# Keys per head in place of queries times the keys' weights, and scores of two heads on the two halves of TensorE's rows

## The chip, the cores and the metric

The kernel runs on one core of one Trainium2 chip. The metric is the device time of one execution in microseconds (us), taken as the median of several runs. The core has five engines that work side by side and wait for one another through semaphores: PE (TensorE, matmuls; its weight loads are listed as PEld), DVE (VectorE), ACT (ScalarE), POOL (GpSimd) and SP (SyncE, which issues most DMAs). Matmuls write to PSUM, which has eight banks of 128 rows x 512 words here; the other operands lie in SBUF.

## What is computed

One decoder layer on 1024 rows of width 1024: a gated network (SwiGLU), a token mixer, and a second gated network, each with a residual and a layer norm. The change lies in the mixer's attention, and in the first network where it prepares the mixer's weights. In the reference:

```python
proj = h @ w_in
q, c, qi, ki, wi, z = jnp.split(proj, SPLITS, axis=-1)   # q: 8 heads x 64
c = _rmsnorm(c, kv_norm_g)                               # latent keys, 128 wide
q_abs = jnp.einsum('blhd,hcd->blhc', q, w_uk) * 64 ** -0.5
sc = jnp.einsum('bqhc,bqkc->bqhk', q_abs, c_sel)         # the 256 keys that the indexer picks
p = jax.nn.softmax(sc, axis=-1)
o_lat = jnp.einsum('bqhk,bqkc->bqhc', p, c_sel)
att = jnp.einsum('bqhc,hcd->bqhd', o_lat, w_uv)
```

The selection is carried out as a bias: each row's 256th largest indexer score is found bit by bit (top-k), and keys below it get a bias of -2^100, so that the softmax runs over all keys up to the causal limit. The score of a head is q (64 wide) times `w_uk` (64 x 128) times c (128 wide); the product may be taken from either side.

## The kernel before

Numbers are kept to about 22 bits by splitting each operand in a high and a low part (`split`, L84: ACT copies the rounded high part, DVE subtracts it to get the low part) and adding three products: high x high, high x low, low x high (`mm3`, L148). `mm2` (L698) does the same with two products where one operand has its high and low part stacked on the 128 rows.

The instructions of an engine are put in order by a planner with a model of their times. It takes what is ready, the earlier in the program first, and can bring a later instruction far forward if its buffer is free. Buffers come from pools: `page` (21 of 128 x 1024 words), `big` (15 of twice that size; `large` and `both` take from it), `w` (2, taken by `raw`), and in PSUM `one` (4 single banks) and `two` (2 double banks). Buffers of a pool are given out in the order of the program, and a buffer is free again when the last reader is done.

The first network runs over 11 groups of hidden columns; a group has five to seven products of 24 matmuls (`product`, L314). From group 2 on, each quarter of a product takes one step of `make_parts` (L99). This generator loads 29 blocks of mixer weights one after another into `w` buffers, splits them on ACT and DVE and stores the parts to HBM. A network's own weights for group g + 1 are loaded while group g runs (L341).

The mixer (L1078) then projects. For the queries, `queries` (L959) projects four heads' columns at a time (`proj_t`) and `stack` (L689) puts a head's high part on one half of the rows and, by a DMA that POOL issues, its low part on the other half. Heads 0 to 3 are done before the product of the gated part with the output weights, heads 4 to 7 behind it. `latent` (L748) norms the latent keys, splits them (`ch`, `cl`) and transposes them (`cT`); its transposes stand behind the last queries. `q_abs` (L967) multiplies the stacked queries with `wuk` and splits the result over the buffers of `act` (eight `big` buffers, no longer needed by then).

The attention (L1015) goes over 16 jobs: pairs of row blocks 0 to 3, in each two groups of four heads, in each the two blocks. For a job, `softmax` (L978) runs per head: three matmuls per chunk of up to 512 keys into a double bank, one DVE reduction that adds the bias and finds the maximum (L993), one exponential with its sum (L995), a reciprocal, and a scaling on POOL (L997). Two heads' `p` share a `big` buffer. Then `attend` (L1000) takes the job before: for each block of keys four transposes of `p`, a split, and three matmuls with the latent keys into `ol`. Behind each two jobs `heads` (L1026) multiplies with `wuv`. The output weights `wo` (four `big` buffers) are loaded behind the ninth job (L1066). Top-k steps are pumped between all of these (`pump`); blocks 4 to 7 end their top-k with an equality mask `eq`, a scan `rank` and an update of the bias (L874 to L885).

Of the kernel before, what the change touches and what calls it, by code (L numbers as in the profile page):

```python
# [34 lines left out]
class Net:  # L35
# [63 lines left out]
    def make_parts(self):  # L99
# [9 lines left out]
        todo += [("wuk", flat(ins["w_ukT"]))]  # L109
# [146 lines left out]
    def ffn(self, name, w13, w2, begin, meanwhile, load_acc, norm, after, side=iter(())):  # L256
# [57 lines left out]
        def product(g, m, ps, start=True):  # L314
            now = plan.index((g, m))
            for k in range(4):
# [12 lines left out]
                if g > 1 and now > 2 * EARLY:  # L329
                    next(side, None)  # L330
# [322 lines left out]
    def w_uk(self):  # L653
        self.wuk = self.load_w("wuk", "wuk", (P, NH, P))

# [142 lines left out]
    def topk(self, blocks, plan):  # L798
# [64 lines left out]
        for i in sorted(blocks):  # L863
# [12 lines left out]
            eq = self.page("eq", (P, 1024), BF16)[:, :n]  # L876
            rank = self.page("rank")[:, :n]
# [81 lines left out]
    def queries(self, j):  # L959
        w = self.load_t(j)  # L960
        two = [self.page("q", dt=F32R) for _ in range(2)]
        lo = self.page("ql", dt=F32R)
        for h in range(2):
            self.stack(two, self.proj_t(w, 4 * h, 4), lo, slice(h * HALF, (h + 1) * HALF))
        return two

    def q_abs(self, q):  # L967
        self.w_uk()
        for h in range(2):
            for head in range(NH):  # L970
                ps = self.bank("qa")
                self.mm2(ps, q[head][:, h * HALF : (h + 1) * HALF], [x[:, head] for x in self.wuk], True)
                if PAR["QA"][8 * h + head]:
                    self.split_far(ps, *self.act_cols(4 * h, 4, head))
                else:
                    self.split(ps.rearrange("p (t c) -> p t c", t=4), *self.act_cols(4 * h, 4, head))

    def softmax(self, i, head):  # L978
        nc, V = self.nc, self.nc.vector
        s = (i + 1) * P  # L980
        n, w = self.chunks(s)
        ps = self.banks("sc")
        for j in range(n):
            ks = slice(j * w, (j + 1) * w)
            self.mm3(ps[:, j * HALF : j * HALF + w], self.act_tile(i, head), (self.cT[0][:, ks], self.cT[1][:, ks]), True, True)
        if head % 2 == 0:
            self.pp = self.large("p", (P, 2, 1024), F32)
        p = self.pp[:, head % 2]
        m, l = self.small("m", 1), self.small("l", 1)
        view = ps.rearrange("p (j c) -> p j c", j=2)[:, :n, :w]  # L990
        pv = p[:, : n * w].rearrange("p (j c) -> p j c", j=n)
        bv = self.bias[i].rearrange("p (j c) -> p j c", j=n)
        V.tensor_tensor_reduce(pv, view, bv, -1.0, 3.0e38, ALU.add, ALU.min, m)  # L993
        p = p[:, :s]
        nc.scalar.activation(p, p, AF.Exp, bias=m, scale=-1.0, accum_out=l)  # L995
        V.reciprocal(l, l)
        self.engine(PAR["PN"][head % 4]).tensor_scalar(p, p, l, 0.0, ALU.mult, ALU.add)  # L997
        return p
# [16 lines left out]
    def attention(self, x1, norm, after):  # L1015
# [10 lines left out]
        def heads(pair, hg):  # L1026
            if hg == 0:
                attT[pair] = [self.page("at", (P, 4, 2, P), F32R) for _ in range(2)]
# [26 lines left out]
        for n, job in enumerate([(pair, hg, b) for pair in PAR["O"] for hg in range(2) for b in range(2)]):  # L1055
# [4 lines left out]
            for hh in range(4):  # L1060
                ready[job].append(self.softmax(2 * pair + b, 4 * hg + hh))
# [16 lines left out]
    def mixer(self, x1, tail, norm, after):  # L1078
# [54 lines left out]
        q = []  # L1133
        for j in range(2):
            q.extend(self.queries(j))
            for i in range(2):
                self.to_gmT(4 + 2 * j + i)
            self.pump(PAR["Q"][j])
        wo = self.load_wout(1)
        for t in range(NT):  # L1140
# [5 lines left out]
            self.pump(PAR["W"][t])  # L1146
        for j in range(2, 4):
            q.extend(self.queries(j))
            self.pump(PAR["Q"][j])
            if PAR["L"] == j:  # L1150
                self.latent(craw)
        if PAR["L"] == 4:
            self.latent(craw)
        self.q_abs(q)
# [31 lines left out]
def layouts(i):  # L1186
# [23 lines left out]
    uk = i["w_uk"][0].transpose(2, 0, 1)  # L1210
# [23 lines left out]
```

## Time and profile before

| | us |
|---|---|
| median of 3 runs | 1782.01 (1781.88 to 1782.98) |
| profiled execution | 1782.18 |
| its span | 1780.5 |
| PE busy | 1728.8 (97%) |
| DVE busy | 1330.2 (75%) |
| ACT busy | 792.0 (44%) |
| POOL busy | 394.1 (22%) |

The profile is taken on one execution. A busy share is an average over stages with different limits: the first network runs from 0 to about 640 us, the mixer to about 1150, the second network to the end. A matmul's own row gives the time from its start to its last output, 0.39 us for 512 columns, and such rows overlap; what a stream of them costs is read from the distance of their starts. The granted clock of PE is a share of 2.4 GHz; it has two levels, 1.0 and 0.5 of that, and a stretch shows a mean. Idle time in brackets is that of the engine just before the instruction, with what ended it.

### The profile page before, as it was taken

The page shows a single profiled execution, that of the slowest core. Times are in us where ns is not written, and L with a number is a line of the kernel's source. Part 1 is how long each engine was busy: PE and PEld are TensorE (multiplying, and loading weights), DVE is VectorE, ACT ScalarE, POOL GpSimd, SP SyncE. Part 2 cuts the span into 40 slices and gives each one's busy share as a digit, 9 for nine tenths or more (in the row PEclk, how much of TensorE's full clock was granted, in tenths as well). Part 3 has the DMA queues.
Part 4 walks back from the last instruction along what each step waited for, and adds up shares of the span by engine and source line. Part 5 has one row for each costly group of instructions (what it writes and reads, how often), then busy time and mean ns, then how long its engine had stood idle before and what let it go on. Part 6 is the DMA issues. An engine that isn't in the chain of part 4 may idle for free.

```text
span 1780.5 us, 22284 instructions
## 1 busy us (share of the span) xinstructions
PE 1728.8 (97%) x8056; PEld 1449.9 (81%) x8056; DVE 1330.2 (75%) x2213; ACT 792.0 (44%) x1328; POOL 394.1 (22%) x287
## 2 busy tenths in 40 slices
PE   8989999999999999999978999999999999999997
PEld 6878888888888889998866888888788888888886
DVE  5778886765895864699889877877877555589586
ACT  5433333333654524568687662452313222354551
POOL 0004332222000460011246421100423222200036
PEclk9999999999999999999999999999999999999999
DMA  7458777758545342225412006435443322753532
GB/s 285 154 213 318 256 262 276 280 204 305 192 122 173 107 184 95 96 84 198 169 36 95 1 1 212 154 119 188 157 178 121 136 89 89 288 195 118 181 101 83
DMA packets 90141, 289.96 MB, mean 163 GB/s; under 512 B 9136, under 2 KB 9648, under 8 KB 85680
## 3 DMA queue, kind: packets, MB, share of 16 engines
q1 hardware_dynamic: 82496, 253.12, 40.1%
q10 hardware_dynamic: 5616, 32.54, 4.6%
q0 software_dynamic: 1920, 2.89, 0.8%
q8 instruction: 63, 1.03, 0.2%
q14 instruction: 46, 0.38, 0.1%
HBM read 195.94 MB, written 89.69 MB: 160 GB/s over the span
## 4 chain that ended last, share of the span: by engine, by line
PE 71%; DVE 7%; ACT 4%; DMA 2%; issue 2%; POOL 1%; SPq 0%; POOLq 0%; ACTq 0%; DVEq 0%
PE ab L151 11%; PE ab L153 11%; PE ab L152 11%; PE y L152 5%; PE y L153 5%; PE y L151 5%; PE z L153 3%; PE z L152 3%; PE z L151 3%; ACT act L828 2%; PE pN L153 2%; PE pN L151 2%; PE pN L152 2%; PE tr L1006 1%; PE lg L702 1%
## 5 line engine op out<-in xcount | busy, mean ns | idle before, releaser
L151 PE MATMUL ab<-xs,hi 128*128 128x512 f32 x1232 | 482.4, 392 | 18.4 <-DVE c L415 6.7
L152 PE MATMUL ab<-xs,hi 128*128 128x512 f32 x1232 | 481.2, 391 | 0.0
L153 PE MATMUL ab<-xs,lo 128*128 128x512 f32 x1232 | 481.0, 391 | 0.0
L151 PEld LDWEIGHTS ab<-xs,hi 128*128 128x128 f32 x1232 | 232.6, 189 | 69.7 <-issue 12.5
L152 PEld LDWEIGHTS ab<-xs,hi 128*128 128x128 f32 x1232 | 232.6, 189 | 48.9 <-DVE xs L88 0.4
L153 PEld LDWEIGHTS ab<-xs,lo 128*128 128x128 f32 x1232 | 232.5, 189 | 48.6
L88 POOL TENSOR_TENSOR lo<-w,hi 128x1024 fp32r<-128x1024 f32 x54 | 137.9, 2553 | 568.6 <-ACT hi L87 531.2
L87 ACT ACTIVATE hi<-w 128x1024 fp32r<-128x1024 f32 (+1 forms) x134 | 137.6, 1040 | 160.4 <-DVE w L290 126.6
L88 DVE TENSOR_TENSOR lo<-w,hi 128x1024 fp32r<-128x1024 f32 (+1 forms) x80 | 94.7, 1195 | 42.4 <-ACT hi L87 41.9
L88 DVE TENSOR_TENSOR a<-hid,a 128x512 fp32r<-128x512 f32 x132 | 93.3, 707 | 24.2 <-ACT a L87 24.0
L87 ACT ACTIVATE a<-hid 128x512 fp32r<-128x512 f32 x132 | 82.0, 621 | 53.9 <-DMA hid<-f 50.2
L153 PE MATMUL z<-b,a 128*128 128x512 f32 x264 | 102.7, 389 | 0.0
L152 PE MATMUL y<-b,a 128*128 128x512 f32 x264 | 102.7, 389 | 0.0
L153 PE MATMUL y<-b,a 128*128 128x512 f32 x264 | 102.7, 389 | 0.0
L152 PE MATMUL z<-b,a 128*128 128x512 f32 x264 | 102.7, 389 | 0.0
L151 PE MATMUL z<-b,a 128*128 128x512 f32 x264 | 102.5, 389 | 0.0
L88 DVE TENSOR_TENSOR b<-w,b 128x512 fp32r<-128x512 f32 x110 | 77.1, 701 | 34.0 <-ACT b L87 33.8
L828 ACT ACTIVATE act<-score,tk 128x768 int8<-128x768 f32 (+2 forms) x93 | 87.0, 935 | 34.2 <-DVE tk L840 27.7
L151 PE MATMUL y<-b,a 128*128 128x512 f32 x264 | 102.0, 389 | 0.0
L87 ACT ACTIVATE b<-w 128x512 fp32r<-128x512 f32 x110 | 68.4, 622 | 51.9 <-PE z L153 38.5
L348 ACT ACTIVATE h<-c 128x512 f32<-128x512 f32 x34 | 21.4, 631 | 152.8 <-DVE c L415 103.3
L592 POOL TENSOR_TENSOR xacc<-xacc,T 128x512 f32<-128x512 f32 x8 | 13.0, 1652 | 333.8 <-DVE T L565 333.8
(264 smaller groups left out, 3586.7 us busy)
## 6 DMA issues: line engine op xcount, KB each, us to landing
w<-in_ffn_w_dram SPq DMA_DIRECT2D x110, 512.0 KB, 6.3
hid<-f SPq DMA_DIRECT2D x60, 512.0 KB, 3.8
w<-in_ffn_w_dram SPq DMA_DIRECT2D x22, 1024.0 KB, 10.3
made<-made ACTq DMA_DIRECT2D x17, 1024.0 KB, 6.3
f<-h SPq DMA_DIRECT2D x32, 512.0 KB, 3.6
f<-c SPq DMA_DIRECT2D x22, 512.0 KB, 3.1
wo<-made SPq DMA_DIRECT2D x8, 1024.0 KB, 6.9
xr<-x_spill SPq DMA_DIRECT2D x16, 512.0 KB, 5.6
```

Source lines behind the costliest of these rows:

```text
L87: nc.scalar.activation(hi, src, AF.Copy)
L88: (eng or nc.vector).tensor_tensor(lo, src, hi.bitcast(F32), ALU.subtract)
L151: mm(out, a[0], b[0], start=start, stop=False, skip_group_check=skip)
L152: mm(out, a[0], b[1], start=False, stop=False, skip_group_check=skip)
L153: mm(out, a[1], b[0], start=False, stop=stop, skip_group_check=skip)
L348: nc.scalar.activation(t, c[:, 0], AF.Silu)
L592: nc.gpsimd.tensor_tensor(acc[j][:, HALF:], acc[j][:, HALF:], T[j], ALU.add)
L702: self.nc.tensor.matmul(out, l, r, start=n == 0, stop=n == 1)
L828: nc.scalar.activation(out, s, AF.Sign, bias=fj, scale=-1.0, accum_out=val[:, j : j + 1])
L1006: nc.tensor.transpose(pt[:, hh * P : (hh + 1) * P], ps4[hh][:, j * P : (j + 1) * P], self.ident)
```

## The change

- `queries` no longer stacks: it only splits a projection, and pair j of heads gives one high and one low array, in which head 2j lies on rows 0 to 63 and head 2j + 1 on rows 64 to 127. For j above 1 the two share a `big` buffer.
- A new function `keys` multiplies the latent keys with `w_uk` (laid out so that again two heads share the 128 rows; half as many words to split and store) and splits the result: four pairs, one `big` buffer each. `q_abs`, `w_uk` and the `far` splits are gone.
- `softmax` works on a pair of heads. For each chunk of keys it issues six matmuls, alternately on rows 0 to 63 and 64 to 127, into two double banks (or, up to 512 keys, the two banks of one).
- `latent` stands ahead of the last two query projections.
- `eq` and `rank` take `w` buffers in place of pages; the attention outputs of pairs 0 and 1 take `big` buffers.
- The steps of `make_parts` begin with group 4 in place of group 2.

```diff
-                if g > 1 and now > 2 * EARLY:
+                if g > 3 and now > 2 * EARLY:
                     next(side, None)
...
-            eq = self.page("eq", (P, 1024), BF16)[:, :n]
-            rank = self.page("rank")[:, :n]
+            eq = self.raw("eq").bitcast(BF16)[:, :n]
+            rank = self.raw("rank")[:, :n]
...
     def queries(self, j):
         w = self.load_t(j)
-        two = [self.page("q", dt=F32R) for _ in range(2)]
-        lo = self.page("ql", dt=F32R)
+        q = self.both("q") if j > 1 else [self.page("q", dt=F32R) for _ in range(2)]
         for h in range(2):
-            self.stack(two, self.proj_t(w, 4 * h, 4), lo, slice(h * HALF, (h + 1) * HALF))
-        return two
+            s = slice(h * HALF, (h + 1) * HALF)
+            self.split(self.proj_t(w, 4 * h, 4), q[0][:, s], q[1][:, s])
+        return q
-    def q_abs(self, q):
...
+    def keys(self):
+        w = self.load_w("wuk", "wuk", (P, 4, P))
+        self.k = [self.both("k") for _ in range(4)]
+        for j in range(4):
+            for h in range(2):
+                s = slice(h * HALF, (h + 1) * HALF)
+                ps = self.bank("k")
+                self.mm3(ps, [x[:, j] for x in w], [x[:, s] for x in self.cT], True, True)
+                self.split(ps, *(x[:, s] for x in self.k[j]))
-    def softmax(self, i, head):
+    def softmax(self, i, j):
...
+        two = [self.banks("sc") for _ in range(n)]
+        view = [(x if n == 2 else two[0][:, e * HALF : (e + 1) * HALF]).rearrange("p (j c) -> p j c", j=n)[:, :, :w] for e, x in enumerate((two * 2)[:2])]
+        for c in range(n):
+            ks = slice(c * w, (c + 1) * w)
+            for m, (a, b) in enumerate(((0, 0), (0, 1), (1, 0))):
+                for e in range(2):
+                    r = slice(64 * e, 64 * e + 64)
+                    nc.tensor.matmul(view[e][:, c], self.q[j][a][r, tl], self.k[j][b][r, ks], start=m == 0, stop=m == 2)
+        pp = self.large("p", (P, 2, 1024), F32)
...
-                attT[pair] = [self.page("at", (P, 4, 2, P), F32R) for _ in range(2)]
+                if pair < 2:
+                    attT[pair] = self.both("at", (P, 4, 2, P))
+                else:
+                    attT[pair] = [self.page("at", (P, 4, 2, P), F32R) for _ in range(2)]
...
+        self.latent(craw)
         for j in range(2, 4):
-            q.extend(self.queries(j))
+            self.q.append(self.queries(j))
             self.pump(PAR["Q"][j])
-            if PAR["L"] == j:
-                self.latent(craw)
...
-        self.q_abs(q)
+        self.keys()
         self.w_uv()
```

## Rows read from the trace of the kernel before

**Rows 1.** Part 1 of the page: busy us, share, instructions, of two engines.
```profile
PE 1728.8 (97%) x8056; PEld 1449.9 (81%) x8056; DVE 1330.2 (75%) x2213; ACT 792.0 (44%) x1328; POOL 394.1 (22%) x287
```
**Rows 2.** Windows: stretch, its length, busy time of each engine, clock, DMA.
```profile
core 0: us, PE busy (x) PEld busy (x) DVE busy (x) ACT busy (x) POOL busy (x), PEclk, DMA share, GB/s
905.00:917.00 12.00, 3.88 (x18) 2.77 (x17) 10.96 (x28) 10.31 (x19) 5.17 (x7) 0.81 0.22 44
917.00:966.00 49.00, 41.40 (x216) 32.18 (x215) 43.91 (x141) 39.15 (x105) 30.42 (x37) 0.98 0.07 18
966.00:1084.00 118.00, 114.78 (x684) 99.55 (x684) 93.76 (x189) 77.45 (x150) 38.31 (x39) 1.00 0.13 44
1500.00:1600.00 100.00, 100.00 (x443) 82.81 (x442) 69.81 (x96) 41.87 (x67) 12.23 (x5) 1.00 0.58 211
120.00:130.00 10.00, 6.38 (x29) 4.94 (x27) 5.71 (x5) 1.79 (x2) 0.00 (x0) 1.00 0.52 209
130.00:140.00 10.00, 8.40 (x25) 6.70 (x26) 8.94 (x6) 4.84 (x6) 6.79 (x3) 0.66 0.56 204
```
**Rows 3.** What PE waited for, 640 to 1160 us: total, times, longest.
```profile
PE qa L702 <- DVE ql L694: 8.1, 2, 5.4
PE sc L151 <- DVE m L993: 4.3, 8, 1.3
```
**Rows 4.** Timeline, 909 to 917 us: start, duration, instruction, idle time before.
```profile
909.89 0.73 PE L702 MATMUL qa<-q,wuk 128*128 128x512 f32 x2 [2.70 <-DVE ql L694]
...
911.32 1.23 DVE L88 TENSOR_TENSOR cl<-c,ch 128x1024 fp32r<-128x1024 f32 x1 [0.42 <-ACT ch L87]
...
915.30 0.69 DVE L694 TENSOR_TENSOR ql<-pT,q 128x512 fp32r<-128x512 f32 x1
...
916.04 1.22 PE L702 MATMUL qa<-q,wuk 128*128 128x512 f32 x2 [5.42 <-DVE ql L694]
```
**Rows 5.** The chain that ended last, 966 to 1084 us, by line.
```profile
by line: PE tr L1006 20.0%; PE ol L151 11.6%; PE ol L152 11.2%; PE ol L153 11.1%; PE sc L151 9.1%; PE sc L153 8.8%; PE sc L152 8.8%; PE at L151 2.2%; DVE pT L88 2.0%; PE at L153 2.0%; PE at L152 2.0%; DVE p L993 1.9%; DVE rank L880 1.6%; AC
```
**Rows 6.** Groups by line and form, 905 to 1150 us: busy us, mean ns.
```profile
L88 DVE TENSOR_TENSOR pT<-tr,pT 128x512 fp32r<-128x512 f32 x72 | 48.2, 684 | 11.4 <-ACT pT L87 11.2
...
L993 DVE CUSTOM_DVE_ANT_0 p<-sc,bias 128x1024 f32<-128x1024 f32 x8 | 9.8, 1221 | 3.1 <-PE sc L153 2.0 <-PE tr L1006 1.0
...
L995 ACT ACTIVATE p<-p,m 128x1024 f32<-128x1024 f32 x8 | 9.2, 1153 | 4.2 <-DVE l L996 2.4 <-DVE m L993 1.7
...
L997 POOL TENSOR_SCALAR p<-p,l 128x1024 f32<-128x1024 f32 x8 | 9.0, 1126 | 12.3 <-DVE l L996 12.3
...
L88 DVE TENSOR_TENSOR act<-qa,act 128x512 fp32r<-128x512 f32 x13 | 8.9, 687 | 0.9 <-ACT act L87 0.6
...
L993 DVE CUSTOM_DVE_ANT_0 p<-sc,bias 128x640 f32<-128x640 f32 x8 | 6.5, 812 | 0.0
```
**Rows 7.** Timeline of PE, 1004 to 1008 us, transposes and scores of blocks 5 and 6.
```profile
1004.01 0.60 PE L1006 MATMUL tr<-ident,p 128*128 128x128 f32 x4
1004.37 0.42 PE L151 MATMUL sc<-cTh,act 128*128 128x384 f32 x1
1004.63 0.34 PE L152 MATMUL sc<-cTl,act 128*128 128x384 f32 x1
1004.81 0.35 PE L153 MATMUL sc<-cTh,act 128*128 128x384 f32 x1
...
1005.72 0.37 PE L152 MATMUL sc<-cTl,act 128*128 128x448 f32 x1
1005.93 0.37 PE L153 MATMUL sc<-cTh,act 128*128 128x448 f32 x1
```
**Rows 8.** Timeline of SP's queue, 955 to 980 us.
```profile
963.09 9.42 SPq L145 DMA_DIRECT2D wo<-made  x4
```
**Rows 9.** Timelines of SP's queue, DVE and PE, 75 to 140 us.
```profile
82.02 20.28 SPq L116 DMA_DIRECT2D made<-in_w_inT_dram  x3
...
124.19 1.23 DVE L287 TENSOR_TENSOR S<-w,w 128x1024 f32<-128x1024 f32 x1 [7.29 <-DMA w<-in_ffn_w_dram]
...
131.60 0.76 PE L151 MATMUL ab<-xs,hi 128*128 128x512 f32 x1 [5.22 <-DVE c L415]
```

More of the change, by code (lines that the diff above doesn't have):

```diff
@@ L651, in gate_consts @@
         nc.sync.dma_start(self.glg[:, 1], ins["gmlp_ln_b"].partition_broadcast(P))
-    def w_uk(self):
-        self.wuk = self.load_w("wuk", "wuk", (P, NH, P))
     def w_uv(self):
@@ L960, in queries @@
         w = self.load_t(j)
-        two = [self.page("q", dt=F32R) for _ in range(2)]
-        lo = self.page("ql", dt=F32R)
+        q = self.both("q") if j > 1 else [self.page("q", dt=F32R) for _ in range(2)]
         for h in range(2):
-            self.stack(two, self.proj_t(w, 4 * h, 4), lo, slice(h * HALF, (h + 1) * HALF))
-        return two
-    def q_abs(self, q):
[L968 to L976, printed above, removed]
-    def softmax(self, i, head):
+            s = slice(h * HALF, (h + 1) * HALF)
[11 more added lines that the diff above has]
+    def softmax(self, i, j):
         nc, V = self.nc, self.nc.vector
@@ L981, in softmax @@
         n, w = self.chunks(s)
[L982 to L998, printed above, removed]
+        tl = slice(i * P, (i + 1) * P)
+        two = [self.banks("sc") for _ in range(n)]
[7 more added lines that the diff above has]
+        pp = self.large("p", (P, 2, 1024), F32)
+        out = []
+        for e in range(2):
+            p = pp[:, e]
+            m, l = self.small("m", 1), self.small("l", 1)
+            pv = p[:, : n * w].rearrange("p (j c) -> p j c", j=n)
+            bv = self.bias[i].rearrange("p (j c) -> p j c", j=n)
+            V.tensor_tensor_reduce(pv, view[e], bv, -1.0, 3.0e38, ALU.add, ALU.min, m)
+            p = p[:, :s]
+            nc.scalar.activation(p, p, AF.Exp, bias=m, scale=-1.0, accum_out=l)
+            V.reciprocal(l, l)
+            nc.gpsimd.tensor_scalar(p, p, l, 0.0, ALU.mult, ALU.add)
+            out.append(p)
+        return out
     def attend(self, i, hg, ps4, olat, pending):
@@ L1059, in attention @@
             ready[job] = []
-            for hh in range(4):
-                ready[job].append(self.softmax(2 * pair + b, 4 * hg + hh))
+            for j in range(2):
+                ready[job] += self.softmax(2 * pair + b, 2 * hg + j)
             self.pump(PAR["A"][4 * pair + 2 * hg + b])
@@ L1132, in mixer @@
         self.gate(1, vn1)
-        q = []
+        self.q = []
         for j in range(2):
-            q.extend(self.queries(j))
+            self.q.append(self.queries(j))
             for i in range(2):
@@ L1146, in mixer @@
             self.pump(PAR["W"][t])
+        self.latent(craw)
         for j in range(2, 4):
-            q.extend(self.queries(j))
+            self.q.append(self.queries(j))
             self.pump(PAR["Q"][j])
-            if PAR["L"] == j:
-                self.latent(craw)
-        if PAR["L"] == 4:
-            self.latent(craw)
-        self.q_abs(q)
+        self.keys()
         self.w_uv()
```

5 lines of the change are left out of this document (2 added, 3 removed).

## The prediction

> **What bounds the kernel now.** The shares of busy time were read first. PE is busy for 1728.8 of 1780.5 us and DVE for 1330.2 [rows 1], so time is won only where PE idles, or where PE's own work shrinks and nothing else comes late in its place. The windows then give the stages around the change, and three of them matter [rows 2]. From 905 to 917 us, between the last query projection and the first scores, PE is busy for 3.9 of 12 us at a mean granted clock of 0.81. From 917 to 966 (scores and attention of blocks 0 to 3) PE has 41.4 of 49 us and DVE 43.9. From 966 to 1084 (blocks 4 to 7) PE has 114.8 of 118 us and DVE 93.8. For scale, a stretch in which PE does nothing but 128x512 products holds 443 matmuls in 100 us, so one costs 0.226 us in a stream [rows 2], whatever longer duration its own row shows.
>
> The waits say what the hole is: the product of the queries with the keys' weights (`qa`) waited 8.1 us in two pieces for `ql`, the low part of the queries [rows 3]. The timeline shows the two pieces: `qa` sat idle 2.70 us before 909.89 and 5.42 us before 916.04, where it followed the DVE subtraction at 915.30 by a fraction of a us; DVE and ACT were full of top-k steps in between. The pair at 916.04 took 1.22 us against 0.73 us for the pair before it [rows 4]: PE had idled, and the granted clock of 0.81 is a mean of the two levels, 1.2 and 2.4 GHz. In the stage from 966 on, the chain that ended last is PE: the three lines of the scores alone hold 9.1 + 8.8 + 8.8 = 26.7% of 118 us, 31.5 us [rows 5].
>
> **The change part by part.** *Queries.* The stacking goes: for each of 8 half projections one 64-row ACT copy and two DMAs issued by POOL (16 in all). What stays is one ACT copy and one DVE subtraction. All of it sits beside PE's projections except in the last projection, where it is the 8.1 us hole. Nothing of the new kernel asks PE to wait there: `keys` needs only the latent transposes, which the change puts ahead of the last two projections, and the scores of the first pair need queries that were ready long before. I count the hole as gone, 8.1 us, and 0.5 us for the pair at the lower clock.
>
> *Keys for queries times weights.* 32 `qa` matmuls go and 24 `k` matmuls come (4 pairs x 2 halves x 3), 8 x 0.226 = 1.8 us less PE work. On DVE 13 subtractions (8.9 us) go and 8 come, at 0.684 us for the same shape 5.5 us [rows 6]. The latent subtraction at 911.32 (1.23 us, [rows 4]) moves ahead into a stage where PE is late. What is late next from 905 to 966 is DVE: today 10.96 + 43.91 = 54.9 us of 61, afterwards 54.9 - 8.9 + 5.5 - 1.2 = 50.3. In 61 - 8.6 = 52.4 us it would be 96% full. So 8.6 us is about all that this stage can give; the bounds are 5.1 us (if DVE stays at today's 90%, 55.9 us) and 10.7 us (DVE never idle).
>
> *Scores on two halves.* The matmul count stays: chunks x 3 x 8 heads, 48 for each of blocks 4 to 7. Today each uses all 128 rows of PE. The spacing of two starts is 0.18 us at 384 columns and 0.21 at 448 [rows 7], 0.226 at 512, and about 0.148 at 320 by the same slope: 48 x (0.148 + 0.177 + 0.205 + 0.226) = 36 us of PE work in the last stage. No row shows a matmul on half of the rows. The bounds are that two such matmuls take turns (36 us, nothing gained) and that they stream together (18 us). I take 18: the nearest row is one full matmul, which today streams as many rows and columns in one spacing as the pair does together, and the pair's outputs lie in different PSUM banks. The Trainium skill, TensorE: Matmul & The Clock Gate, section LDWEIGHTS, puts a weight load at 128 columns over 1.2 GHz, 107 ns whatever its rows; as an estimate from that page two loads cost 0.213 us for a pair, so the narrow pairs would not get below that and the 18 us would be 21. No row here separates this, since a load now always lies beside a full matmul.
>
> Each run of half-row matmuls changes what PE does. The nearest row is a change from transposes to scores: the first matmul then takes 0.26 us to the next start instead of 0.18 [rows 7], 0.08 us more. With 16 pairs in the last stage and a change at each end this is 32 x 0.08 = 2.6 us; the upper bound is one full pass of the pipeline, 0.34 - 0.18 = 0.16 us, at 64 changes (each run of six on its own): 10 us. The Trainium skill, TensorEngine Tiling (Array Packing), section Key Properties, speaks against the change here: changing the tiling mode drains TensorE. By it the 10 us would stand in place of the 2.6; the 0.08 us row shows that a change costs something, not that it is a drain.
>
> PE work from 966 on is then 114.8 - 18 + 2.6 = 99.4 us, and DVE keeps 93.8.
>
> *Buffers.* This is what stands against the gain. Of 15 `big` buffers the new kernel holds 4 for keys, 2 for the late queries, 1 for `wuv`, 2 for the attention outputs of pairs 0 and 1, and, from the ninth job on, 4 for `wo` (today loaded from 963.09 on, just as block 4 starts, [rows 8]). Two are left for `p`, which is one job of four heads; today it is 15 - 1 - 4 - 4 = 6. So jobs 9 to 15 can fill `p` only after the job before has been transposed. One job's softmax, from the first reduction to the last scaled head, is for block 7 four reductions 4 x 1.22, the second pair's matmuls 6 x 0.226, one exponential 1.15 and one scaling 1.13 [rows 6]: 8.6 us. For block 4, by the reduction's 0.812 / 1.221, it is 5.7, and the seven jobs add up to 51.5 us (6.7 + 5.7 + 6.7 + 7.6 + 8.6 + 7.6 + 8.6). The transposes follow, and what trails them lies under the next softmax: four PSUM banks let about three groups of splits and value products trail. A job's turn is so 8.6 + 1.7 (a first group: four transposes 0.60 [rows 7], then ACT and DVE, estimated at 1.1 together) + 5 x 0.684 = 13.7 us for block 7 and 5.7 + 1.7 + 2 x 0.684 = 8.8 for block 4; jobs 9 to 15 take 81 us, and about 95 with job 8 and the tail. PE (99), DVE (94) and this turn (95) are then nearly level, and three that wait on one another will not keep PE at today's 97%. I take 93%: 99.4 / 0.93 = 107 us in place of 118, a gain of 11. The bounds are 94 us (DVE never idle) and 133 us (below, as a rival).
>
> `eq` and `rank` move into the two `w` buffers, so each top-k end waits for the one before; the blocks that come last, 6 and 7, are needed only from job 12 on. I cost it at nothing, hidden by jobs 8 to 11; without that cover it is one pass of DVE over a block, which the reduction of the same width puts near 1.2 us.
>
> *Splits begin with group 4.* Today the first weight load of these splits is issued at 82.02 us, and with the later ones it competes with the group's own loads: DVE idles 7.29 us for `w` before 124.19, and PE then waits 5.22 us before 131.60 [rows 9]. The windows 120 to 130 and 130 to 140 hold 29 and 25 matmuls, the second at a clock of 0.66, where 10 us at full speed hold 44.3: (15.3 + 19.3) x 0.226 = 7.8 us lost [rows 2]. But the splits' place in the program is group 2, and the wait at 131.60 (on L415) still belongs to group 1: the first load went out some 50 us or more ahead of its place, with nothing but a free `w` buffer to wait for, and the buffers are the same after the change. I take 0 and keep -7.8 us as a bound. On the other side, if the splits do start ten products later (240 x 0.226 = 54 us), they end as much later, nearer to the network's second half.
>
> **The sum.** The profiled execution took 1782.18 us (span 1780.5 and 1.7 around it), 0.2 above the median of 1782.01. 1782.2 - 8.6 - 11 = 1762.6 us.
>
> **The rivals.** (C) The splits do start late enough that the stall around 131.60 is gone too: 1762.6 - 7.8 = 1754.8. For it speaks that the stall follows a late DMA; against it, the early issue at 82.02. (E) The three limits of the last stage overlap better, 97% for PE (102.5 us) or DVE's 94: 1758 to 1750. (B) The two halves take turns: PE keeps its 115 us, the stage its 118, and only the hole is won: 1773.6. Nothing in the trace speaks for or against it, as no half-row matmul is there. (F) As B, with a full pass lost at 64 changes, 10 us of which the present 3 us of idle time hide a part: 118 + 7 = 125, so 1780.6, no change. This is also how it would look if the change did not do what it says. (D), on the other side: the two `p` buffers make softmax and attention strictly alternate. Then PE's work without scores, 114.8 - 36 = 79, and the softmax turns of 51.5 add up, with 2.6 for changes, to 133 us, 15 more than today: 1782.2 - 8.6 + 15 = 1788.6, slower. It decides if less than about a third of each softmax lies over the trailing splits and products of the job before; for it speaks the count of buffers, against it that four PSUM banks let three groups trail.
>
> **How the numbers follow.** My forecast 0.40, C 0.17, E 0.10, B 0.13, F 0.06, D 0.14. A measurement of this kernel can tell about 0.2%, 3.6 us, from no change. Faster is the forecast, C, E and B, 0.80; the same is F, 0.06; slower is D, 0.14. The range leaves out D and F, 0.20, and reaches on the low side to C and E together with DVE never idle, 1750 - 7.8 = 1742, rounded in to 1743; its upper end of 1779 lies above B.
>
> **What would show it.** Right: no wait of PE for a query between the last projection and the first scores, and no clock below 1.0 there; starts of half-row matmuls in pairs, a pair in about 0.23 us at 512 columns; the stage from block 4 on near 107 us with PE busy well below 97%; waits of DVE's reductions for a `p` buffer, that is for transposes, from the ninth job on. Wrong: half-row starts 0.2 us apart each (B); the stage over 120 us with DVE and PE both below 75% (D); no late `w` load before group 2 in the first network (C). The prediction fails most easily in the last stage, where the gain is a difference of limits that lie close together.

## The result, and the profile after

The changed kernel takes 1796.88 us (median of 4 runs, 1794.75 to 1798.86) beside 1782.43 us for the kernel before on the same chip: a ratio of 1.0082, 95% interval 1.0069 to 1.0094. It is 14.5 us slower; the forecast was 19.4 us faster. The profiled execution has a span of 1795.0 us.

Part 1 of the page, to be read beside [rows 1]: PE is busy 11.8 us longer than before, with 8 matmuls fewer.

```profile
PE 1740.6 (97%) x8048; PEld 1444.7 (80%) x8048; DVE 1328.6 (74%) x2208; ACT 782.2 (44%) x1309; POOL 387.5 (22%) x268
```

Windows of the kernel after, beside [rows 2]. The first line is the hole of before (3.88 of 12 us at clock 0.81): it is full now, at full clock. The last stage runs from 966 to 1098 instead of 1084 (the first product of the output projection starts at 1098.5, before at 1084.5). PE is busy for 95% of it, a little more than the 93% of the forecast, but over 132 us in place of 107; DVE is busy for 65%, where it had been 79%.

```profile
core 0: us, PE busy (x) PEld busy (x) DVE busy (x) ACT busy (x) POOL busy (x), PEclk, DMA share, GB/s
905.00:917.00 12.00, 12.00 (x58) 9.02 (x57) 11.12 (x31) 8.93 (x17) 5.55 (x2) 1.00 0.00 1
917.00:966.00 49.00, 36.69 (x195) 24.82 (x191) 44.97 (x134) 33.32 (x92) 35.35 (x39) 0.83 0.00 1
966.00:1098.00 132.00, 125.71 (x669) 97.46 (x670) 85.65 (x179) 76.23 (x146) 33.51 (x35) 0.96 0.16 55
```

The waits of PE, 640 to 1160 us, beside [rows 3]: the wait for `ql` is gone, and none as large has come. The 14 us can't be found in this list.

```profile
PE sc L989 <- DVE m L997: 6.4, 6, 2.1
PE ol L151 <- ACT pT L87: 4.5, 7, 0.8
PE sc L989 <- DVE tk L879: 2.2, 1, 2.2
PE tr L763 <- DVE xr L952: 2.0, 1, 2.0
```

The timeline of PE shows the keys right behind the last query projection (compare [rows 4]) and, in the last stage, the half-row matmuls of block 6 (compare [rows 7]). The six of one head stand as a run, then a value product, then the six of the other head. Six take 1.49 us, the same 0.2 us per start as full rows had.

```profile
910.26 0.39 PE L153 MATMUL pT<-act,wT 128*128 128x512 f32 x1
910.49 0.39 PE L151 MATMUL k<-cTh,wuk 128*128 128x512 f32 x1
...
1051.42 1.49 PE L989 MATMUL sc<-k,q 64*128 64x448 f32 x6
1052.85 0.49 PE L151 MATMUL ol<-pT,ch 128*128 128x512 f32 x1
1053.27 1.48 PE L989 MATMUL sc<-k,q 64*128 64x448 f32 x6
1054.68 0.50 PE L152 MATMUL ol<-pT,ch 128*128 128x512 f32 x1
1055.03 0.40 PE L153 MATMUL ol<-pT,cl 128*128 128x512 f32 x1
1055.26 0.60 PE L1011 MATMUL tr<-ident,p 128*128 128x128 f32 x4
```

SP's queue and PE in the first network, beside [rows 9]: the first load of the splits is issued at 81.47 us (82.02 before), and the stall at L415 stays.

```profile
81.47 11.14 SPq L116 DMA_DIRECT2D made<-in_w_inT_dram  x2
...
PE ab L151 <- DVE c L415: 4.9, 1, 4.9
```

Three places in time divide the loss. The query projections end at 910.7 us (906.3 before), the first scores start at 912.6 (917.1), the output projection at 1098.5 (1084.5); from there to the end both kernels take 696 us. So 4.4 us come ahead of the attention, 8.9 us are won in the hole, and 18.5 us are lost between the first scores and the output projection.

A fourth place says where. The first scores of block 4, 320 columns wide, start at 965.22 us before and at 956.71 after. The windows run from there to the output projection, before and after:

```profile
965.22 0.31 PE L151 MATMUL sc<-cTh,act 128*128 128x320 f32 x1
965.20:1084.50 119.30, 116.08 (x692) 100.76 (x691) 94.65 (x193) 78.53 (x151) 39.11 (x39) 1.00 0.14 47
```
```profile
956.71 0.52 PE L989 MATMUL sc<-k,q 64*128 64x320 f32 x2 [0.51 <-DVE m L997]
956.70:1098.50 141.80, 134.20 (x718) 104.25 (x719) 93.99 (x195) 82.49 (x161) 36.08 (x38) 0.96 0.15 53
```

At block 4 the changed kernel is still 8.5 us ahead. It has put off some matmuls of blocks 0 to 3 (9 transposes, 7 value products and 12 products with `wuv`, 3.8 us by their usual distances). Behind this place it loses 22.5 us, with the same work on DVE.

### The profile page after: what moved, and what is told of

It reads as the page before. It is cut to its first block, busy times and chain, and to the rows that moved or that the text cites. A ratio compares the mean times of both kernels' runs of the same rounds, so it can differ in the third digit from the quotient of the medians.

```text
span 1795.0 us, 22187 instructions
## 1 busy us (share of the span) xinstructions
PE 1740.6 (97%) x8048; PEld 1444.7 (80%) x8048; DVE 1328.6 (74%) x2208; ACT 782.2 (44%) x1309; POOL 387.5 (22%) x268
## 4 chain that ended last, share of the span: by engine, by line
PE 71%; DVE 7%; DMA 3%; POOL 3%; ACT 2%; issue 2%; SPq 0%; POOLq 0%; ACTq 0%; DVEq 0%
PE ab L151 11%; PE ab L152 11%; PE ab L153 11%; PE y L151 4%; PE y L153 4%; PE y L152 4%; PE z L153 2%; PE z L151 2%; PE z L152 2%; PE pN L153 2%; PE pN L151 2%; PE sc L989 2%; PE pN L152 2%; PE tr L1011 2%; PE pT L151 1%
## 5 line engine op out<-in xcount | busy, mean ns | idle before, releaser
L151 PE MATMUL ab<-xs,hi 128*128 128x512 f32 x1232 | 481.8, 391 | 17.4 <-DVE c L415 6.8
L152 PE MATMUL ab<-xs,hi 128*128 128x512 f32 x1232 | 480.9, 391 | 0.0
L153 PE MATMUL ab<-xs,lo 128*128 128x512 f32 x1232 | 480.7, 390 | 0.0
L152 PEld LDWEIGHTS ab<-xs,hi 128*128 128x128 f32 x1232 | 232.3, 189 | 48.3 <-DVE xs L88 0.4
L153 PEld LDWEIGHTS ab<-xs,lo 128*128 128x128 f32 x1232 | 232.2, 189 | 48.4 <-DVE lo L88 0.2
L87 ACT ACTIVATE hi<-w 128x1024 fp32r<-128x1024 f32 (+1 forms) x134 | 137.6, 1039 | 161.8 <-DVE w L290 124.1
L152 PE MATMUL y<-b,a 128*128 128x512 f32 x264 | 102.7, 389 | 0.0
L153 PE MATMUL y<-b,a 128*128 128x512 f32 x264 | 102.7, 389 | 0.0
L152 PE MATMUL z<-b,a 128*128 128x512 f32 x264 | 102.7, 389 | 0.0
L153 PE MATMUL z<-b,a 128*128 128x512 f32 x264 | 102.7, 389 | 0.0
L816 DVE TENSOR_SCALAR_CACHE_REDUCE dve<-score,tk 128x640 int8<-128x640 f32 (+3 forms) x96 | 84.5, 880 | 0.4
## 6 DMA issues: line engine op xcount, KB each, us to landing
w<-in_ffn_w_dram SPq DMA_DIRECT2D x22, 1024.0 KB, 11.3
```

Of the source, the lines that this page charges most:

```text
L87: nc.scalar.activation(hi, src, AF.Copy)
L151: mm(out, a[0], b[0], start=start, stop=False, skip_group_check=skip)
L152: mm(out, a[0], b[1], start=False, stop=False, skip_group_check=skip)
L153: mm(out, a[1], b[0], start=False, stop=stop, skip_group_check=skip)
L816: V.tensor_scalar(self.marks("dve", s.shape[-1]), s, f, None, ALU.is_lt, ALU.add, accum_out=val[:, j : j + 1])
```

## The experiments

Times are medians in us; each ratio is against the kernel before on the same chip. "The stage" is the time from the end of the query projections to the start of the output projection. For it, each matmul's time from its start to the next start was added up from the single rows of the trace, idle gaps of PE apart (before, e10 and e12 have 8 transposes of latents, 1.0 us, among theirs):

```
kernel            time    ratio [95%]              stage   scores  transposes  values  PE idle
before          1782.4    1                        178.1    56.6     28.2       54.4     18.9
after           1796.9    1.0082 [1.0069, 1.0094]  187.8    54.9     36.3       61.6     18.6
e1_alternate    1793.5    1.0053 [1.0036, 1.0069]  186.8    42.2     39.7       63.9     24.8
e4_full_rows    1788.5    1.0034 [1.0023, 1.0044]  180.5    57.4     30.4       57.7     19.1
e5_wo_last      1787.4    1.0025 [1.0015, 1.0035]  179.4    55.5     33.4       60.5     13.5
e6_alt_wo       1776.1    0.9966 [0.9954, 0.9979]  168.2    41.7     33.0       60.6     16.4
e7_full_wo      1777.3    0.9972 [0.9961, 0.9982]  169.7    57.4     28.7       54.4     13.3
e10 (before)    1794.0    1.0068 [1.0051, 1.0084]  188.5    57.3     30.4       55.6     24.7
e11_same_half   1792.4    1.0055 [1.0040, 1.0070]  183.9    64.7     34.0       60.2      7.9
e12 (before)    1782.6    1.0002 [0.9992, 1.0011]  178.3    57.1     28.5       54.0     17.9
```

**Do the halves meet? (e1)**

```
+        with self.tc.manual_schedule(engines={mybir.EngineType.PE}):
             for c in range(n):
                 ...
                         nc.tensor.matmul(view[e][:, c], ...)
```

> The changed kernel, with the score matmuls of one softmax call held in the order of the program on PE, so that the two heads' halves alternate from matmul to matmul; nothing else differs. Theory 'order': for blocks 4 to 7 the planner issues the six matmuls of one head as a run and the six of the other later, so that the halves seldom meet. If that is why nothing was gained, the starts of half-row matmuls come in pairs, a pair in about 0.23 us at 512 columns and 0.2 at 448, the 39 us of score matmuls in blocks 4 to 7 fall to about 20, and the kernel takes 1780 to 1785 us. Rival 'turns': the two halves can't stream together, the spacing of two starts stays 0.2 us at 448 columns, and the time stays at 1795 to 1799 us. Rival 'limit': the starts pair up, but the p buffers and DVE set the stage, and the time stays within 4 us of 1797.

Measured: 1793.5 us. The starts do pair up, as forecast in the prediction (0.20 us a pair at 448 columns, 0.23 at 512), and the score matmuls fall from 54.9 to 42.2 us. But PE's idle time and the lower clock (0.76 to 0.90 in windows of 20 us from 980 to 1040 us) take nearly all of it: the stage is 1 us shorter. 'Order' is right about the halves and wrong about the time; 'limit' is what the time says. 'Turns' falls.

**What the p buffers cost (e5, e12, e10).** The first two edits are one number, on either kernel; the third holds four buffers in the kernel before.

```
e5, e12:  -'WJ': 8   +'WJ': 16
e10:       wo = self.load_wout(0)
          +held = [self.large("held", (P, 2, 1024), F32) for _ in range(4)]
          +for x in held: nc.sync.dma_start(x[:, 0, :64], ...)
           ...
          +if n == 15:
          +    for x in held: nc.gpsimd.tensor_tensor(..., x[:, 0, :1], ready[job][3][:, :1], ALU.add)
```

> The changed kernel, with the load of the output weights at the end of the attention in place of behind its ninth job, so that four more big buffers stay free for p in jobs 9 to 15. Theory 'p buffers': with two p buffers the softmax of jobs 9 to 15 waits for the transposes of the job before; freed, the stage from block 4 on falls from about 127 us to 118 or less, and the output projection starts with a wait of up to 10 us for its weights (4 loads of 9.7 us beside one another, if nothing else hides them): 1788 to 1797 us, with the wait named. Rival 'no limit': the p buffers are not what PE waits for, the stage stays within 2 us, and the wait for the weights comes on top: 1797 to 1806 us.

> The kernel before, with its output weights loaded at the end of the attention: the edit of e5 alone, on the other kernel. Theory 'p buffers': before has six p buffers in its last jobs, four more change nothing, 1781 to 1784 us. Rival 'the load itself': the loads of the weights in the middle of the attention disturb it (9.4 us on the queue), or more p buffers help here as well: 1770 to 1778 us; e5's gain would then not be the change's own loss.

> The kernel before, with four of its big buffers taken from the ninth job of the attention to the last softmax (four small loads of 32 KB and, at the end, four operations of one column on GpSimd that read them). Everything else is as before: full rows, queries times weights. It leaves two buffers for p from there on, as the changed kernel has. Theory 'p buffers': the softmax of a job then waits for the transposes of the job before, and the attention behind the queries grows from 178 us by 9 to 16 us: 1791 to 1799 us. Rival 'only with halves': the lack of p buffers hurts only where the order of the half-row runs makes the softmax late; here it costs 0 to 3 us: 1782 to 1786 us.

Measured: e5 1787.4 us, 9.5 less than the changed kernel, and PE doesn't wait for the weights; e12 1782.55 (1.0002, interval 0.9992 to 1.0011), nothing; e10 1794.0, 12 us more than before. All three say 'p buffers', though e5 lies 0.6 us below the band of that theory and the wait for the weights that it expected did not come. The lines of the score matmuls carry the first and last start: after, e5, then L153 of before, e10 and e12.

```profile
L989 PE MATMUL sc<-k,q x288: 271/373/763, 912.6 to 1076.4; 64*128 64x384 f32 x36, 64*128 64x512 f32 x34, 64*128 64x448 f32 x26, 64*128 64x256 f32 x24
```
```profile
L989 PE MATMUL sc<-k,q x288: 273/373/789, 912.2 to 1053.1; 64*128 64x384 f32 x38, 64*128 64x512 f32 x38, 64*128 64x256 f32 x24, 64*128 64x320 f32 x22
```
```profile
L153 PE MATMUL sc<-cTh,act x96: 278/338/399, 919.9 to 1048.4; 128*128 128x384 f32 x24, 128*128 128x512 f32 x24, 128*128 128x256 f32 x16, 128*128 128x320 f32 x16
```
```profile
L153 PE MATMUL sc<-cTh,act x96: 277/338/400, 917.8 to 1075.5; 128*128 128x384 f32 x24, 128*128 128x512 f32 x24, 128*128 128x256 f32 x16, 128*128 128x320 f32 x16
```
```profile
L153 PE MATMUL sc<-cTh,act x96: 277/341/447, 918.3 to 1039.2; 128*128 128x384 f32 x24, 128*128 128x512 f32 x24, 128*128 128x256 f32 x16, 128*128 128x320 f32 x16
```

With two buffers the last scores start at 1075 to 1076 us in either kernel (at 1069 in e4, below), with six or more at 1039 to 1053. The order of PE's instructions shows why no wait does: with two buffers the planner puts the scores of a job behind the transposes of the job before. Scores (S512:6 is six score matmuls of 512 columns) and transposes (t:4 is four) as they stand on PE, all else left out:

```
before, last jobs:  ... S512:6 t:4 S512:6 t:4 S512:6 t:4 S512:6 S448:6 t:12 S448:12 t:8 S448:6 t:4 S512:12 t:8 S512:12 t:108
e10, last jobs:     ... t:22 S448:12 t:1 S512:6 t:1 S512:6 t:26 S512:12 t:1 S448:6 t:1 S448:12 t:1 S448:6 t:1 S512:12 t:32 S512:6 t:4 S512:6 t:52
```

In the windows from 1000 to 1050 us (after, e10, then before) PE is busy for 46.5 and 44.7 of 50 us and DVE for 31 with two buffers; with six, before, PE is at 50.0 and DVE at 39.1.

```profile
1000.00:1050.00 50.00, 46.47 (x225) 34.90 (x225) 31.22 (x68) 26.97 (x52) 13.12 (x14) 0.91 0.00 1
```
```profile
1000.00:1050.00 50.00, 44.68 (x250) 36.64 (x251) 31.17 (x67) 28.15 (x53) 11.18 (x13) 1.00 0.00 1
```
```profile
1000.00:1050.00 50.00, 50.00 (x284) 43.51 (x283) 39.10 (x84) 34.49 (x67) 18.53 (x18) 1.00 0.00 1
```

**Both limits at once (e6, e11).** e6 is e1 and e5 together; e11 is e6 with one line changed, so that both heads use the first half (it leaves out the scores of the odd heads):

```
-r = slice(64 * e, 64 * e + 64)
+r = slice(0, 64)
```

> The two edits of e1 and e5 together: score matmuls of the two heads alternating on PE, and the output weights loaded at the end of the attention. Alone, the first cut the score matmuls from 55 to 42 us but PE only idled more (1793.5 us), and the second gave 10 us (1787.4 us). Theory 'two limits': the saved PE time was hidden by the lack of p buffers; with both, the stage from the last query projection to the output projection, 179 us in e5, loses 8 to 12 us more, and the kernel takes 1776 to 1780 us, faster than the kernel before by 0.2 to 0.4%. Rival 'chain of the softmax': the turn of reduction, exponential, scaling, transposes and splits is the limit with six p buffers as well, or the lower clock takes the gain: 1785 to 1789 us, as e5.

> e6 (halves alternate, output weights loaded last), with both heads' matmuls on the rows of the first half: it leaves out the scores of the odd heads (they get those of the even ones); count, order and width of the matmuls stay. Theory 'halves': e6 gained over e5 because neighbours lie on different halves; on the same half each start comes 0.2 us after the one before at 448 columns and 0.23 at 512, the score matmuls take 55 us again in place of 42, and the kernel takes 1785 to 1789 us. Rival 'fewer changes': e6 gained because twelve matmuls in one run change the mode less often than two runs of six; then the same half costs little, 1776 to 1780 us.

Measured: e6 1776.1 us, faster than either kernel (0.9966 of before): 'two limits'. The alternation that gave 3.4 us with two p buffers gives 11.3 with six, and the buffers that gave 9.5 us give 17.4. e11 takes 1792.4 us, 3.4 us beyond what 'halves' expected. The timelines of PE show one softmax call of block 6 in e6, in e11 and in e7 (below):

```profile
1010.17 1.50 PE L990 MATMUL sc<-k,q 64*128 64x448 f32 x12
```
```profile
1038.72 2.70 PE L990 MATMUL sc<-k,q 64*128 64x448 f32 x12
```
```profile
1027.19 1.48 PE L989 MATMUL sc<-k,q 128*128 128x448 f32 x6
```

Twelve on alternating halves take what six take on full rows, or six on one half; twelve on one half take 2.70 us. In these runs the halves stream together where neighbours in the order lie on different ones.

**What half rows cost elsewhere (e4, e7).** A change of mode is the step from full-row to half-row matmuls or back. Both runs put the score matmuls over all rows, which leaves out the separation of the two heads; e7 has the late load of e5 as well:

```
-nc.tensor.matmul(..., self.q[j][a][r, tl], self.k[j][b][r, ks], ...)
+nc.tensor.matmul(..., self.q[j][a][:, tl], self.k[j][b][:, ks], ...)
```

> The changed kernel, with each score matmul over all 128 rows in place of 64: it leaves out the separation of the two heads (both get the sum of their scores); the count, order and widths of the matmuls stay. Theory 'change of mode': each run of half-row matmuls costs about 0.1 us where it begins and 0.1 us in the matmul behind it; some 50 runs make 8 to 10 us of PE time in the scores and transposes, and with full rows the kernel would be 6 to 10 us faster than the changed one, 1787 to 1791 us, with the clock drop of 921 to 938 us still there. Theory 'clock': the half-row matmuls are what lowers the clock in 921 to 938 us, and with full rows the clock stays at 0.9 or more there: 5 us more. Rival 'overlap': where two halves do meet, in blocks 0 to 3, full rows lose that overlap (about 8 us of matmuls), which takes back what the changes of mode cost: 1795 to 1799 us.

> The two edits of e4 and e5 together: score matmuls over all 128 rows (which leaves out the separation of the two heads), and the output weights loaded at the end of the attention. It prices what half rows cost where p buffers are no limit. Theory 'change of mode and clock': in e5 the stage from the last query projection to the output projection holds 8.3 us of time lost to the lower clock and some 6 us of changes of mode; without both it is 179 - 10 or less, and the kernel takes 1775 to 1779 us. Rival: e4's gain came from the softmax's turn (scores that end sooner), which e5 has already given: 1785 to 1788 us.

Measured: 1788.5 and 1777.3 us, both in the band of 'change of mode'; but in e4 the clock from 920 to 940 us is 0.91, as only 'clock' had expected, without the further 5 us of that theory. Together with e5 the two runs price both costs, here by the time from the first scores of block 4 to the output projection (before: 119.3 us):

```
             two p buffers     six p buffers
half rows    141.8 (after)     133.1 (e5)
full rows    132.9 (e4)        123.6 (e7)
```

Each costs about 9 us, whichever way the other stands. Half rows with two p buffers also bring the clock down in this stage, to 0.96 over the 132 us from 966 on; in e4, e5 and e7 it is 1.00 from 960 us on.

Against e6, e7 has 16 us more of score matmuls, and 10 us less of transposes and value products, so that they end within 1.2 us of one another. The single rows at full clock give the price of a run of six at 448 columns, from the start of the last transpose ahead of it to the start of the second value product behind it: 0.03 + 1.30 + 0.23 = 1.56 us on full rows (e7), 0.20 + 1.41 + 0.34 = 1.95 on half rows (e5). That is 0.39 us for a run that saves nothing itself; between two value products it is 0.24 + 1.23 + 0.23 = 1.70 and 0.33 + 1.41 + 0.34 = 2.08. So a change costs about 0.19 us, two to a run, and the matmuls on both sides of it share the cost; e6 has 36 runs, the changed kernel 40. The fence from 1051.42 us on shows a part: L152 behind a run starts 0.35 us ahead of L153, and L153 0.23 us ahead of the transposes. Twelve alternating matmuls take 0.20 + 1.43 + 0.34 = 1.97 us (e6), twelve on full rows 0.03 + 2.52 + 0.23 = 2.78 (before): 0.8 us won, where half of the run would have been 1.26.

**Where half rows pay, and the clock (e13, e14).**

```
-r = slice(64 * e, 64 * e + 64)
+r = slice(0, P) if n == 1 else slice(64 * e, 64 * e + 64)     (e13; n == 2 in e14)
```

> e6 (halves alternate, output weights loaded last), with full rows for the score matmuls of blocks 0 to 3 (for these it leaves out the separation of the two heads); blocks 4 to 7 keep their halves. Theory 'clock': half rows are what lowers the granted clock between 920 and 940 us, 0.53 and 0.62 in e6; with full rows there it stays at 0.85 or more, as in e4, and the stage of blocks 0 to 3 ends 3 to 5 us earlier: 1771 to 1773 us. Rival 'top-k': DVE sets that stage (9.75 of 10 us busy from 920 to 930 in e6), so that PE's clock costs nothing: the clock rises, and the time stays at 1774.5 to 1778 us. Rival 'idle time': the clock falls because PE has little to do there, whatever the rows: it stays near 0.55 and so does the time.

> e6, with full rows for the score matmuls of blocks 4 to 7 (for these it leaves out the separation of the two heads); blocks 0 to 3 keep their halves. In e6 the halves save about half of 34 us of score matmuls there. Theory 'halves pay late': PE is busy for 94% from 1000 to 1050 us, so most of the 17 us less some 6 us for changes of mode (32 changes of 0.1 us at each end) is lost again: 1782 to 1788 us. Rival 'given back': the turn of softmax and splits is the limit there, and half rows bring nothing: 1774.5 to 1779 us.

Measured: e13 1778.0 us (0.9974, 0.9963 to 0.9984), e14 1780.8 us (0.9994, 0.9984 to 1.0004). The windows from 920 to 940 us, e6 and e13:

```profile
920.00:940.00 20.00, 16.18 (x71) 10.56 (x69) 19.05 (x56) 11.94 (x42) 15.12 (x18) 0.57 0.00 1
```
```profile
920.00:940.00 20.00, 14.28 (x71) 11.43 (x72) 18.72 (x60) 13.58 (x44) 14.74 (x19) 0.91 0.00 1
```

With the same 71 matmuls, and PE less busy, full rows keep the granted clock at 0.91 where half rows see 0.57, that is mostly the lower of its two levels, 1.2 GHz. Two half rows that overlap also keep PE streaming for less time, but e11, where they follow one another and PE is busy for 18.7 of the 20 us, shows the same 0.57:

```profile
920.00:940.00 20.00, 18.74 (x66) 13.80 (x66) 19.18 (x57) 11.30 (x40) 14.43 (x17) 0.57 0.00 1
```

So it is the half rows, not idle time or the overlap, with which the clock falls there. But the time doesn't follow: DVE is busy for 94 to 95% of that stretch, and e13 is no faster. 'Top-k' holds. In blocks 4 to 7 half rows are worth 4.7 us, below 'halves pay late' (6 us or more) and above 'given back' (3 us at most): e13 and e14 give the score matmuls of these blocks 26.4 us on alternating halves and 38.5 on full rows, 12 us less, of which the transposes and value products of the same stage, 7 us longer in e6 than in e7 (5 us longer than in e14), take back about half.

**Why the queries end late (e2, e8, e9).**

```
e2:  the line  self.latent(craw)  behind  queries(2), queries(3)  again
e8:  -eq = self.raw("eq").bitcast(BF16)[:, :n]     +eq = self.page("eq", (P, 1024), BF16)[:, :n]
     -rank = self.raw("rank")[:, :n]               +rank = self.page("rank")[:, :n]
e9:  e6 and e8 together
```

> The changed kernel, with the latent transposes back behind the last two query projections, where the kernel before had them. Theory 'bank': placed ahead of the queries, the transposes wait for a PSUM bank and hold PE's queue, which cost 4.5 us by the end of the query projections; moved back, the queries end at 906 us again in place of 910.3, the keys wait for the split of the latents (1 to 2 us), and the kernel takes about 1793 us. Rival 'same work': the wait was late work of ACT and DVE that comes up again somewhere else, and the keys now wait for it: 1796 to 1798 us, with a hole of 4 us or more ahead of the keys.

> The changed kernel, with eq and rank of the top-k ends back in pages of their own, as the kernel before has them. It asks what makes the query projections end 4.5 us late. In the changed kernel ACT stands 5.16 us for the load of a late xr page before 864.57, DVE idles 4.52 us behind it, and the top-k steps and the evictions between them run late. Theory 'w buffers': the two w buffers tie the ends of the top-k together, and the planner's order of pages follows from it; undone, the queries end near 906 us and the kernel takes 1791 to 1794 us. Rival 'pages': the late xr load comes from the other moves (queries' halves in pages and big buffers, latents ahead), and the undone edit leaves the end of the queries at 910 us or later: 1795 to 1800 us.

> The edits of e6 (halves alternate, output weights loaded last) and that of e8 (eq and rank of the top-k ends in pages again). In e8 the queries ended at 905.9 us, 4.8 us earlier than in the changed kernel, but the attention behind them took 197.9 us in place of 187.8. Theory 'p buffers': what was won ahead of the attention was lost because its last jobs wait for p buffers anyway; with these free it stays won, the stage is near 168 us as in e6, and the kernel takes 1770 to 1773 us. Rival 'pages': eq and rank take the pages that pT needs while the last blocks are masked, the attention is longer by some 10 us whatever the p buffers, and the kernel takes 1780 to 1787 us.

Measured: e2 1803.0 us (1.0107, 1.0090 to 1.0124), e8 1799.0 (1.0090, 1.0069 to 1.0111), e9 1776.15 (0.9965, 0.9952 to 0.9978). Neither theory of e2 holds: the queries end at 912.2 us, and PE waits 3.6 us for the last query weights, whose load stands behind the stores of `xr` in SP's queue. With the latents ahead of the queries, in the changed kernel, PE has no such wait there. What starts the delay is seen on ACT and DVE in the changed kernel (timelines):

```profile
864.57 1.06 ACT L943 ACTIVATE xr<-xr 128x1024 f32<-128x1024 f32 x1 [5.16 <-DMA xr<-x_spill]
...
866.37 0.15 DVE L867 TENSOR_SCALAR tk<-tk 128x1 f32<-128x1 f32 x1 [4.52 <-ACT act L866]
```

In e8 that wait for the load is gone and the queries end at 905.9 us: the `w` buffers for `eq` and `rank` are behind it. (This end varies by some 2 us: 908.2 to 911.9 us in the other runs of the changed kernel whose edits lie behind it, 904.3 to 906.3 in before, e10 and e12.) Yet the stage grows to 197.9 us, and in e9, with six p buffers, the queries end 5.3 us earlier than in e6 (904.5 beside 909.8) and the output projection starts at the same 1077.8 us. Both theories of e9 miss (1770 to 1773, 1780 to 1787): being earlier there is worth nothing to the end. What else paces the attention then was not isolated.

**The splits (e3).**

```
-if g > 3 and now > 2 * EARLY:
+if g > 1 and now > 2 * EARLY:
```

> The changed kernel, with the splits' place in the first network at group 2 again, as the kernel before has it. Theory 'no part': the first load of the splits is issued near 82 us in either kernel, the stall of 5 us around 131.6 us stays in both, and the time stays within 3 us of the changed kernel's 1796.9 us. Rival 'delayed splits': group 4 puts the splits' end later, and what follows in the first network or the mixer waits for it: 3 us or more faster with group 2. Rival the other way: group 4 has removed part of the stall, and group 2 is 3 us or more slower.

Measured: 1800.2 us (1.0098, 1.0082 to 1.0113), 3.3 us above the changed kernel, with intervals that overlap. Group 2 is not faster; whether group 4 brings a little these runs can't tell.

## Why the prediction was wrong, point by point

**The hole** was right: from the end of the queries to the first scores 10.8 us became 1.9, 8.9 won against 8.6, and PE runs 12 of 12 us there, at full clock as forecast. e7, with full rows and enough buffers, has a stage of 169.7 us, 8.4 less than before; the whole kernel gains 5.1 us, not 8.6, as its queries end 1.8 us later and what follows the attention takes 2.1 us longer in the profiled execution. The stretch behind the hole was nearly as full on DVE as forecast (44.97 of 49 us, 92% beside 96%). The fall of the clock there, to 0.57 from 920 to 940 us, was not foreseen, but cost nothing that e13 could find.

**The p buffers** are the step that failed first. The count (two left from the ninth job on) and the mechanism stood in the prediction; the size did not. That PE, DVE and this turn are "then nearly level", with 93% for PE and a gain of 11 us, took the trailing splits and products to lie under the next softmax. They do so only in part: e10 puts two p buffers alone at 12 us, e5 takes back 9.5 us, e6 against e1 17.4. This comes nearest to rival D, which had 0.14, but not to its strict alternation: D's sign was DVE and PE both below 75%, and while DVE is at 65%, PE is at 95%. The forecast's own sign was wrong too: DVE's reductions do not wait for a `p` buffer, that is for transposes. The planner knows that there is none, and the limit is in the order that it wrote, as lumps of 22 to 32 transposes between the scores in e10, where before has 4 to 12, not as a wait. That this order costs the time is argued from the windows, where PE and DVE are both less busy; no run changes the order alone.

**The scores on halves** failed in another place than rival B named. That two half matmuls stream as one was right (1.50 us for twelve at 448 columns). But "I take 18" assumed that the planner would keep them side by side. For blocks 4 to 7 each head has a PSUM tile of its own, these come free one after the other, and the planner issues each head's six as soon as it can: the score work stayed at 54.9 us of 56.6, and in blocks 4 to 7 it rose from 37.7 to 40.9. e1 and e11 show it. And where they do alternate the saving in blocks 4 to 7 is 12 us, not 18.

**The change of mode** was priced and counted short: 0.08 us a change was taken, with 0.16 as the bound, and 0.19 was measured; 32 changes were counted in the last stage, where the changed kernel has 28 runs, that is 56 changes (e6 24 runs). 28 runs of 0.38 us are 10.6 us, near the 8.9 that e4 gives back; 2.6 had been taken and 10 was the bound. The row behind it was the wrong one: a first score behind a transpose takes 0.08 us more with full rows as well. The Trainium skill, TensorEngine Tiling (Array Packing), section Key Properties, says that a change of mode drains TensorE. The rows agree in so far as each change costs more than the bound of one pass (0.19 beside 0.16 us); that it is a drain they do not show.

**The queries, `eq` and `rank`.** "I cost it at nothing" was wrong for where the queries end (e8: 4.8 us) and right for the end of e6 and e9 (0.0 us).

**The splits** were right: 0, with the load at 81.47 us and the stall in place.

The losses of the two rivals that had been given 0.13 and 0.14 came together, that of B by another mechanism than its own. The forecast had treated them as cases that exclude one another, so no case and no range held 1796.9. Of the 34 us between forecast and result, 19.6 are what the p buffers and the half rows cost together (changed kernel against e7). Of the rest, 11 are the gain of the last stage that was forecast and that full rows cannot give, and 3.5 are the hole, worth 5.1 us to the whole kernel and not 8.6. Set right as in e6, half rows bring 1.2 us over e7, which lies within the intervals. Their scores save 12 us and not 18, and the transposes and products beside them are 7 us longer, where 2.6 had been taken for all changes. What else keeps e6 from the forecast stays open.

## What to carry to other kernels

Count the buffers that are left to a pipeline at its narrowest point before the saving on any engine is counted: the same alternation was worth 3 us with two buffers and 11 with six. A pairing of instructions that pays only side by side has to be pinned in the program's order, or a planner that frees one operand first will pull it apart. Where two adverse mechanisms don't exclude one another, price them together.

## What the hardware showed that was not expected

Two half-row matmuls run as one even where they are short: in e6 eleven at 320 columns take 1.14 us.

```profile
963.92 1.14 PE L990 MATMUL sc<-k,q 64*128 64x320 f32 x11
```

Their pairs start 0.144 us apart, as single full-row ones do (0.147), and at 256 columns 0.117 us apart. The Trainium skill, TensorE: Matmul & The Clock Gate, section LDWEIGHTS, had led to an estimate of 0.213 us for the two weight loads of a pair, one behind the other. Pairs at 0.117 and 0.144 us do not bear that estimate out, and the loads are no limit here. The Trainium skill, TensorEngine Tiling (Array Packing), section Key Properties, says that different tiles can load weights and multiply in parallel. With that the pairs agree. A matmul on half of the rows alone costs what one on all rows does: 0.203 us at 448 columns for both. And the granted clock fell to 0.57 with half rows, overlapping or not, where full-row matmuls kept 0.91 (e6 and e11, e13).
